# Order at the joints of an FFN: weighted sums ahead of the last gate quarter, half of them on TensorE, a half quarter ahead of the last token block

## The chip, the cores and the metric

The kernel runs on one core of a Trainium2 chip. The metric is the device time of one execution in microseconds (us). The engines are TensorE (PE; its weight loads are listed as PEld), VectorE (DVE), ScalarE (ACT), GpSimd (POOL) and SyncE (SP, which issues most of the DMA transfers).

## The reference

Two layers over 512 tokens of 1024 numbers, all float32. Each layer has a mixer (layer 0: a state-space mixer beside a pooling mixer; layer 1: stick-breaking attention) and then an FFN, which is what the change touches. Cut to what matters:

```
x   = layer_norm(ALPHA * x + mixer(x), ln_mix_g[i], ln_mix_b[i])
ple = (p[i] @ ple_w_proj[i]) * sigmoid(x @ ple_w_gate[i])
ffn = grouped_moe(x, ...)     # 16 SwiGLU experts in 4 groups, best group, best 2 experts in it
x   = layer_norm(ALPHA * x + ffn + ple, ln_ffn_g[i], ln_ffn_b[i])
```

In the mixture of experts each token goes to two experts, and the two results are summed with the weights (gates) that the router gave.

## The kernel before

The tokens stand in four blocks of 128 (`xt[0]` to `xt[3]`), each a tile of 128 x 1024. Every product with a weight is done in three matmuls (`mm3`, lines 87 to 89) on a high and a low part of both operands; the high part of a weight is made by ScalarE (L82) and the low part by VectorE (L83) from a raw tile that SP has loaded. The rows of the trace name the parts of a ring of such tiles `w_0h`, `w_0l`, `w_2l` and so on. Raw weights, the rows `yt` and the tile `yl` share a pool of slots; PSUM has four banks named A, two named B, two named T. A tile waits for the last reader of what stood in its slot or bank. Every engine carries out its instructions in one fixed order, which a list scheduler makes from the order in which the code emits them; nothing overtakes within an engine.

`ffn(layer, last)` goes as follows. For each token block, a POOL DMA writes it to DRAM (`xd`), PE transposes it (L168), and ACT and DVE split the transposed block into the tiles `cath`, `catl` (in layer 1 `oh`, `ol`). `logits` (L794, L795) puts the router's products for all blocks into one bank `pr`, and `route` (from L801 on) turns these on DVE into lists of tokens, gates and an index tile `ixm` (L913). With that index POOL gathers the rows of an expert (L934, tile `xg`), and `load_g` transposes them on PE (L994) and splits them into `g`. `up` and `down` are the two stages of an expert; there are 16.

Beside the experts stand four gate quarters, `gate_parts(c)`, each of 256 columns of the `ple` term and in two halves `b` of two token blocks: 48 matmuls into a bank `pG` (x times the gate weights), a sigmoid on ACT (L964), 12 matmuls into a bank `pB` (p times its weights, `pT`), the product of both on DVE (L968) and its addition to x (L972, L974). Two quarters stand at the start, ahead of the first expert, one among the experts, and the last, c = 3, at the end.

At the end SP loads the experts' results, two per token, from DRAM into `yt` (L1064; one tile of 1 MB for each token block). The last expert doesn't go that way: its result stays in SBUF as `yl` (high part by ACT, L1068, low part by DVE, L1069), and PE brings it to the tokens with a one-hot matrix (L1098, into an A bank). In each half of the last quarter, after the quarter's own work, DVE adds the two weighted `yt` rows of a block (L1085, the weighted sums), then the one-hot product from the A bank (L1100, which also sums up the rows for the layer norm), and `ln_finish` follows (L781 and L784 on DVE, a square on ACT, a power on POOL, L786 and L787 on DVE). In layer 1 alone, blocks 2 and 3 take their weighted sums on PE: four small copies on ACT (L1077) make diagonal matrices `dg` of the gates, and L1094 multiplies them with `yt` into the same bank.

After the first FFN comes the attention layer, which begins with the transposes of the four blocks and the value projection (pA <- w, x2T).

Of the kernel before, what the change touches and what calls it, by code (L numbers as in the profile page):

```python
# [11 lines left out]
AF = mybir.ActivationFunctionType  # L12
OP = mybir.AluOpType
AX = mybir.AxisListType

D = 1024
S = 512
NT = 4
# [3 lines left out]
NE = 16  # L22
CAP = 96
# [3 lines left out]
GATES = (-1, -1, 7, 15)  # L27
# [3 lines left out]
LF = 9  # L31
# [7 lines left out]
class Trunk:  # L39
# [875 lines left out]
    def ffn(self, layer, last):  # L915
        nc, v = self.nc, self.nc.vector
        xt = self.xt
        X = self.cat or self.xt_pair(f"x{layer}T")
        xd = self.dp.tile([S, D], F32, name=f"xd{layer}")
        yd = self.dp.tile([2 * S, D], F32, name=f"yd{layer}")  # L920
        pT = self.pT
        xgs = self.slot(f"xg{layer}").rearrange("p (a d) -> p a d", a=2)
        nc.gpsimd.memset(xgs, 0.0)
        pr = self.bank("B", "pB")
        for i in range(NT):
            nc.gpsimd.dma_start(xd[i * 128:(i + 1) * 128, :], xt[i])
            self.transposes(xt[i], i, X, "TA"[i % 2])
        for i in range(NT):
            self.logits(X, pr, i)
        self.prefetch(self.used + 2 * GATES.count(-1) + LF)  # L930
        self.route(pr, layer)

        def gather(e):
            return nc.gpsimd.indirect_dma_start(  # L934
                out=xgs[:CAP, e % 2, :], out_offset=None, in_=xd[:, :],
                in_offset=bass.IndirectOffsetOnAxis(ap=self.ix[:CAP, e:e + 1], axis=0),
                bounds_check=S - 1, oob_is_err=False)

        def scatter(e, src):
            nc.gpsimd.indirect_dma_start(  # L940
                out=yd[:, :], out_offset=bass.IndirectOffsetOnAxis(ap=self.iy[:CAP, e:e + 1], axis=0),
                in_=src[:CAP], in_offset=None, bounds_check=2 * S - 1, oob_is_err=False)

        with self.tc.issue_after(gather(0).ins):
            scatter(NE - 1, xgs[:, 1, :])
        gather(1)

        def ple(p, i, w):
            ts = slice(i * 128, (i + 1) * 128)
            for k in range(2):  # L950
                self.mm3(p, (pT[:, 0, k, ts], pT[:, 1, k, ts]), w[k], k == 0, k == 1)
# [3 lines left out]
        def gate_parts(c):  # L955
            w = self.weights(LA)
            wp = self.weights(LA)
            cs = slice(c * 256, (c + 1) * 256)
            for b in range(2):
                p = self.bank("A" if c < ng or c == 3 else "B", "pG").rearrange("p (i n) -> p i n", i=2)  # L960
                for i in range(2):
                    self.proj_x(p[:, i], 2 * b + i, X, w)
                sg = self.half4("sg")[:, :512].rearrange("p (i n) -> p i n", i=2)
                nc.scalar.activation(sg, p, AF.Sigmoid)  # L964
                p = self.bank("B", "pB").rearrange("p (i n) -> p i n", i=2)
                for i in range(2):
                    ple(p[:, i], 2 * b + i, wp)
                v.tensor_tensor(sg, sg, p, op=OP.mult)  # L968
                for i in range(2):
                    x = xt[2 * b + i][:, cs]  # L970
                    if c < 3:
                        v.scalar_tensor_tensor(x, x, ALPHA, sg[:, i], op0=OP.mult, op1=OP.add)  # L972
                    else:
                        v.tensor_tensor(x, x, sg[:, i], op=OP.add)  # L974
                    if c == 2:
                        x = xt[2 * b + i][:, 768:]
                        nc.scalar.activation(x, x, AF.Copy, scale=ALPHA)
                yield

        def gate(c):  # L980
            for _ in gate_parts(c):
                pass

        ng = GATES.count(-1)
        for c in range(ng):
            gate(c)

        def load_g(e):
            g = self.slot(f"g{layer}_{e}", F32R)[:, :2 * KB * CAP].rearrange("p (a k t) -> p a k t", a=2, k=KB)
            for hf in range(2):  # L990
                p = self.bank("T", "pT")[:, :4 * CAP]
                for k in range(4):
                    kb = hf * 4 + k
                    nc.tensor.transpose(p[:, k * CAP:(k + 1) * CAP], xgs[:CAP, e % 2, kb * 128:(kb + 1) * 128],  # L994
                                        self.ident[:CAP, :CAP])
                ks = slice(hf * 4, hf * 4 + 4)
                self.split(g[:, 0, ks], g[:, 1, ks], p.rearrange("p (k t) -> p k t", k=4))
            if e + 2 < NE:
                gather(e + 2)
            return g  # L1000

        def up(g, hh, kh, a, pool=False):
            w = self.weights(LA, pool)
            for k in range(4):
                kb = kh * 4 + k
                self.mm3(hh[a][:CAP], (g[:, 0, kb], g[:, 1, kb]), w[k], kb == 0, kb == KB - 1)
# [16 lines left out]
        def down(sT):  # L1023
            for nh in range(2):
# [3 lines left out]
                    self.mm3(py, (sT[:, 0, k], sT[:, 1, k]), w[k], k == 0, k == 3)  # L1028
                yield slice(nh * 512, (nh + 1) * 512), py

        g = load_g(0)
        hh = [self.bank("A", "pA"), self.bank("A", "pA")]
        up(g, hh, 0, 0)
        up(g, hh, 0, 1)
# [3 lines left out]
        for e in range(NE - 1):  # L1038
            LA = 6 if e < 13 else 3
            sg = act(hh)  # L1040
            hh = [self.bank("A", "pA"), self.bank("A", "pA")]
            up(gn, hh, 0, 0)
            sT = turn(sg)
            up(gn, hh, 0, 1)
            ysb = self.half4("ysb")
            for h, py in down(sT):
                nc.scalar.activation(ysb[:CAP, h], py, AF.Copy)  # L1047
            scatter(e, ysb)
            if e == OVER:
                self.overflow(layer, xd, yd)  # L1050
            if e == NE - 3:
                oht = self.last_onehot()
                self.ln_setup("ln_ffn", layer)
            if e in GATES:
                gate(GATES.index(e))
            g = gn
            if e + 2 < NE:
                gn = load_g(e + 2)
            up(g, hh, 1, 0)
            up(g, hh, 1, 1)  # L1060
        yts = []
# [5 lines left out]
        for h, py in down(turn(act(hh))):  # L1067
            nc.scalar.activation(yl[:CAP, 0, h], py, AF.Copy, scale=self.gs[:CAP])  # L1068
            v.scalar_tensor_tensor(yl[:CAP, 1, h], py, self.gs[:CAP], yl[:CAP, 0, h].bitcast(F32),  # L1069
                                   op0=OP.mult, op1=OP.subtract)  # L1070
        st = self.cp.tile([128, NT, 2], F32, tag="st", bufs=2, name=f"st{layer}f")
        onpe = (2, 3) if last else ()
        if onpe:
            dg = self.half4("dg").rearrange("p (x t) -> p x t", x=8)
            for n, i in enumerate(onpe):
                for k in range(2):
                    nc.scalar.activation(dg[:, 2 * n + k], self.ident, AF.Copy, scale=self.gates[:, k, i])  # L1077
        parts = gate_parts(3)
        for b in range(2):
            next(parts)  # L1080
            for i in (2 * b, 2 * b + 1):
                if i in onpe:
                    continue
                for k in range(2):
                    v.scalar_tensor_tensor(xt[i], yts[i][:, k * D:(k + 1) * D], self.gates[:, k, i], xt[i],  # L1085
                                           op0=OP.mult, op1=OP.add)
            for i in (2 * b, 2 * b + 1):
                for nh in range(2):
                    h = slice(nh * 512, (nh + 1) * 512)
                    p = self.bank("A", "pA")  # L1090
                    first = True
                    if i in onpe:
                        for k in range(2):
                            nc.tensor.matmul(p, dg[:, 2 * onpe.index(i) + k],  # L1094
                                             yts[i][:, k * D + nh * 512:k * D + (nh + 1) * 512], start=first, stop=False)
                            first = False
                    for a in range(2):
                        nc.tensor.matmul(p, oht[:CAP, i * 128:(i + 1) * 128], yl[:CAP, a, h], start=first, stop=(a == 1))  # L1098
                        first = False
                    v.scalar_tensor_tensor(xt[i][:, h], p, 1.0, xt[i][:, h], op0=OP.mult, op1=OP.add,  # L1100
                                           accum_out=st[:, i, nh:nh + 1])
                self.ln_finish(xt[i], st[:, i], f"{layer}f{i}")
                if last:
                    nc.sync.dma_start(self.out[i * 128:(i + 1) * 128, :], xt[i])
# [202 lines left out]
```

## Time and profile before

| | |
|---|---|
| median of 3 runs | 1246.93 us (1245.92 to 1250.49) |
| the profiled execution | 1245.8 us |
| its span, first to last instruction | 1244.1 us |
| mean granted TensorE clock | 0.976 |
| busy share PE, DVE, ACT, POOL | 94%, 78%, 60%, 11% |

Idle time of PE is the difference between its busy time and the span. A timeline row gives the start, the time of one or of a merged group, the engine, the line, the operation, what it writes and reads, and in brackets how long the engine stood idle before it and what ended that. Matmuls overlap one another, so the distance of their starts is the pace, not the time of one.

### The profile page before, as it was taken

To read this page: it belongs to the slowest core of one execution; us is meant where nothing else is said; L and a number is where in the kernel's file an instruction comes from. 1 tells how busy PE (TensorE), PEld (TensorE's weight loads), DVE (VectorE), ACT (ScalarE), POOL (GpSimd) and SP (SyncE) were. 2 spreads that over 40 slices of the span, in tenths; PEclk is the share of its full clock that TensorE was granted. 3 is DMA by queue.
4 is the path that set the end of the run, shared out by engine and by line. 5 is a ranking of instruction groups with operands and counts; after the bars stand their busy time and mean duration, and the time that the engine had idled before them with its cause. 6 is when DMAs were issued, how large, how long until landed. Compare 5 with 4: busy or idle time off the path is not lost.

```text
span 1244.1 us, 17404 instructions
## 1 busy us (share of the span) xinstructions
PE 1164.7 (94%) x6463; PEld 891.8 (72%) x6463; DVE 966.0 (78%) x1385; ACT 749.7 (60%) x1059; POOL 136.5 (11%) x150
## 2 busy tenths in 40 slices
PE   6977999999999999987999999998999999998985
PEld 4867779777768776676777767688877768776763
DVE  6997866798886989776576467758599886998765
ACT  4312542688876888742465446523588885888751
POOL 5010021011100110100000000011101110011101
PEclk9988999999999999988999999999999999999998
DMA  7225653599996998952122024434399997999851
GB/s 251 68 79 180 234 217 121 187 371 385 383 379 226 381 387 305 329 227 83 35 67 70 1 69 157 155 143 149 110 359 383 378 373 256 349 388 333 315 216 69
DMA packets 158167, 285.15 MB, mean 229 GB/s; under 512 B 19584, under 2 KB 43664, under 8 KB 157008
## 3 DMA queue, kind: packets, MB, share of 16 engines
q1 hardware_dynamic: 143760, 256.56, 57.9%
q0 software_dynamic: 9568, 25.19, 5.9%
q10 hardware_dynamic: 4736, 2.10, 0.6%
q8 instruction: 56, 0.92, 0.3%
q14 instruction: 47, 0.39, 0.1%
HBM read 272.02 MB, written 20.19 MB: 235 GB/s over the span
## 4 chain that ended last, share of the span: by engine, by line
PE 40%; DVE 8%; DMA 4%; issue 2%; ACT 1%; POOL 0%; POOLq 0%; ACTq 0%; DVEq 0%
PE pA L89 8%; PE pA L88 8%; PE pA L87 8%; DMA xg<-xd,ixm 3%; DVE kw L679 2%; PE pB L89 2%; PE pB L88 2%; PE pB L87 2%; PE pA L691 2%; PE pG L87 1%; PE pG L88 1%; PE pG L89 1%; DVE kw L680 1%; PE pT L686 1%; PE pT L994 1%
## 5 line engine op out<-in xcount | busy, mean ns | idle before, releaser
L83 DVE TENSOR_TENSOR w_0l<-raw,w_0h 128x1024 fp32r<-128x1024 f32 (+1 forms) x233 | 280.0, 1202 | 61.9 <-ACT w_0h L82 57.5
L82 ACT ACTIVATE w_0h<-raw 128x1024 fp32r<-128x1024 f32 (+1 forms) x233 | 242.5, 1041 | 62.4 <-PE pG L89 33.9
L83 DVE TENSOR_TENSOR w_2l<-raw,w_2h 128x1024 fp32r<-128x1024 f32 x205 | 249.8, 1219 | 18.0 <-ACT w_2h L82 17.7
L82 ACT ACTIVATE w_2h<-raw 128x1024 fp32r<-128x1024 f32 x205 | 216.5, 1056 | 52.4 <-PE pA L89 43.1
L87 PE MATMUL pA<-w_0h,g 128*96 128x512 f32 x256 | 104.3, 407 | 2.4 <-ACT g L82 2.4
L88 PE MATMUL pA<-w_0l,g 128*96 128x512 f32 x256 | 100.9, 394 | 1.8 <-DVE w_0l L83 1.8
L89 PE MATMUL pA<-w_0h,g 128*96 128x512 f32 x256 | 101.8, 398 | 0.9 <-DVE g L83 0.9
L89 PE MATMUL pA<-w_2h,g 128*96 128x512 f32 x256 | 101.6, 397 | 0.0
L87 PE MATMUL pA<-w_2h,g 128*96 128x512 f32 x256 | 101.2, 395 | 0.0
L88 PE MATMUL pA<-w_2l,g 128*96 128x512 f32 x256 | 100.9, 394 | 0.0
L940 POOL DMA_INDIRECT yd<-ysb,ixm x30 | 37.7, 1257 | 444.6 <-ACT ysb L1047 422.4
L89 PEld LDWEIGHTS pA<-w_0h,g 128*96 128x96 f32 x256 | 41.2, 161 | 19.9 <-DVE g L83 3.1
L934 POOL DMA_INDIRECT xg<-xd,ixm x32 | 38.9, 1215 | 145.2 <-PE pT L994 91.8
L88 PEld LDWEIGHTS pA<-w_2l,g 128*96 128x96 f32 x256 | 41.6, 163 | 18.0
L89 PEld LDWEIGHTS pA<-w_2h,g 128*96 128x96 f32 x256 | 41.4, 162 | 18.1
L87 PEld LDWEIGHTS pA<-w_0h,g 128*96 128x96 f32 x256 | 41.5, 162 | 17.6 <-ACT g L82 4.6
L87 PEld LDWEIGHTS pA<-w_2h,g 128*96 128x96 f32 x256 | 41.3, 162 | 17.7
L88 PEld LDWEIGHTS pA<-w_0l,g 128*96 128x96 f32 x256 | 41.5, 162 | 17.4 <-DVE w_0l L83 3.8
L87 PE MATMUL pB<-w_0h,sT 128*96 128x512 f32 x128 | 50.9, 397 | 1.2 <-ACT sT L82 1.2
L89 PE MATMUL pB<-w_0h,sT 128*96 128x512 f32 x128 | 51.2, 400 | 0.0
L88 PE MATMUL pB<-w_0l,sT 128*96 128x512 f32 x128 | 50.7, 396 | 0.4 <-DVE w_0l L83 0.4
L679 DVE TENSOR_TENSOR_SCAN kw<-kw 128x128 f32<-128x128 f32 (+3 forms) x64 | 50.3, 813 | 0.9 <-ACT kw L676 0.6
(442 smaller groups left out, 2812.6 us busy)
## 6 DMA issues: line engine op xcount, KB each, us to landing
raw<-in_moe_w_dram SPq DMA_DIRECT2D x192, 1024.0 KB, 10.1
raw<-in_sb_w_qkv_dram SPq DMA_DIRECT2D x12, 1024.0 KB, 9.4
raw<-in_ple_w_gate_dram SPq DMA_DIRECT2D x8, 1024.0 KB, 10.8
yt<-yd SPq DMA_DIRECT2D x8, 1024.0 KB, 7.1
raw<-in_ab_w_out_dram SPq DMA_DIRECT2D x4, 1024.0 KB, 5.7
xd<-x0r POOLq DMA_DIRECT2D x8, 512.0 KB, 4.2
raw<-in_sb_w_out_dram SPq DMA_DIRECT2D x4, 1024.0 KB, 6.1
raw<-in_ab_w_in_dram SPq DMA_DIRECT2D x3, 1024.0 KB, 7.3
```

The lines of the kernel that those rows point to most:

```text
L82: return (self.nc.scalar.activation(hi, src, AF.Copy), (self.nc.gpsimd if pool else self.nc.vector).tensor_tensor(lo, src, hi.bitcast(F32) ...
L83: (self.nc.gpsimd if pool else self.nc.vector).tensor_tensor(lo, src, hi.bitcast(F32), op=OP.subtract))
L87: t.matmul(out, s[0], m[0], start=first, stop=False)
L88: t.matmul(out, s[0], m[1], start=False, stop=False)
L89: t.matmul(out, s[1], m[0], start=False, stop=last)
L679: v.tensor_tensor_scan(rv, rv, rv, 1.0, op0=OP.mult, op1=OP.min)
L680: v.tensor_tensor(sg[:, :n - 1], sg[:, :n - 1], kp[:, 1:n], op=OP.mult)
L686: nc.tensor.transpose(pT[:, ks], sg[:, ks], self.ident)
L691: nc.tensor.matmul(po[s * 64:s * 64 + 64, qs], vs[:, kb, hc:hc + 64], kw[s][:, kb * 128:(kb + 1) * 128], start=(kb == 0), stop=(kb == qb))
L934: return nc.gpsimd.indirect_dma_start(out=xgs[:CAP, e % 2, :], out_offset=None, in_=xd[:, :], in_offset=bass.IndirectOffsetOnAxis(ap=self. ...
L940: nc.gpsimd.indirect_dma_start(out=yd[:, :], out_offset=bass.IndirectOffsetOnAxis(ap=self.iy[:CAP, e:e + 1], axis=0), in_=src[:CAP], in_of ...
L994: nc.tensor.transpose(p[:, k * CAP:(k + 1) * CAP], xgs[:CAP, e % 2, kb * 128:(kb + 1) * 128], self.ident[:CAP, :CAP])
```

## The change

There are four edits, all in `ffn`. At the start, `gate_parts(0)` is opened early: its first half is emitted ahead of the last token block's transposes, each block's logits directly follow its transposes, and the second half comes after the first two gathers. The first half of quarter 1 is emitted ahead of `load_g(0)`, its second half after it. At the end, the weighted sums of blocks 0 and 1 are emitted ahead of quarter 3, and blocks 2 and 3 take theirs on PE in both layers. The second half of quarter 3 puts its `pG` into a B bank.

```
-        pr = self.bank("B", "pB")
-        for i in range(NT):
-            nc.gpsimd.dma_start(xd[i * 128:(i + 1) * 128, :], xt[i])
-            self.transposes(xt[i], i, X, "TA"[i % 2])
-        for i in range(NT):
-            self.logits(X, pr, i)
-        self.prefetch(self.used + 2 * GATES.count(-1) + LF)
-        self.route(pr, layer)
...
-                p = self.bank("A" if c < ng or c == 3 else "B", "pG").rearrange("p (i n) -> p i n", i=2)
+                p = self.bank("A" if c < ng or (c == 3 and b == 0) else "B", "pG").rearrange("p (i n) -> p i n", i=2)
...
         ng = GATES.count(-1)
-        for c in range(ng):
-            gate(c)
+        pr = self.bank("B", "pB")
+        early = gate_parts(0)
+        for i in range(NT):
+            nc.gpsimd.dma_start(xd[i * 128:(i + 1) * 128, :], xt[i])
+            if i == NT - 1:
+                next(early)
+            self.transposes(xt[i], i, X, "TA"[i % 2])
+            self.logits(X, pr, i)
+        self.prefetch(self.used + 2 * ng - 2 + LF)
+        self.route(pr, layer)
...
+        for _ in early:
+            pass
...
+        early = gate_parts(1)
+        next(early)
         g = load_g(0)
+        for _ in early:
+            pass
...
-        onpe = (2, 3) if last else ()
-        if onpe:
-            dg = self.half4("dg").rearrange("p (x t) -> p x t", x=8)
-            for n, i in enumerate(onpe):
+        onpe = (2, 3)
+        dg = self.half4("dg").rearrange("p (x t) -> p x t", x=8)
+        for n, i in enumerate(onpe):
+            for k in range(2):
+                nc.scalar.activation(dg[:, 2 * n + k], self.ident, AF.Copy, scale=self.gates[:, k, i])
+        for i in range(NT):
+            if i not in onpe:
                 for k in range(2):
-                    nc.scalar.activation(dg[:, 2 * n + k], self.ident, AF.Copy, scale=self.gates[:, k, i])
+                    v.scalar_tensor_tensor(xt[i], yts[i][:, k * D:(k + 1) * D], self.gates[:, k, i], xt[i],
+                                           op0=OP.mult, op1=OP.add)
         parts = gate_parts(3)
         for b in range(2):
             next(parts)
-            for i in (2 * b, 2 * b + 1):
-                if i in onpe:
-                    continue
-                for k in range(2):
-                    v.scalar_tensor_tensor(xt[i], yts[i][:, k * D:(k + 1) * D], self.gates[:, k, i], xt[i],
-                                           op0=OP.mult, op1=OP.add)
```

Three places show how the edits move instructions. Line numbers shift with the change: L968 becomes L944, L972 and L974 become L948 and L950, L1069 becomes L1074, L1094, L1098 and L1100 become L1097, L1101 and L1103; the weighted sum keeps L1085.

First, VectorE at the end of the first FFN, from the last weight split of the tail on (`x0r_1245` holds blocks 0 and 1, `yt_0` the rows of block 0). Before:

```order
L83 TENSOR_TENSOR w_0l<-raw_5291,w_0h 128x512
L1069 SCALAR_TENSOR_TENSOR yl_5279<-pB,gs,yl_5279 96x512 x2
L968 TENSOR_TENSOR sg<-sg,pB 128x512
L974 TENSOR_TENSOR x0r_1245<-x0r_1245,sg 128x256 x2
L1085 SCALAR_TENSOR_TENSOR x0r_1245<-yt_0_5271,gates_1696,x0r_1245 128x1024
L1085 SCALAR_TENSOR_TENSOR x0r_1245<-yt_1_5273,gates_1696,x0r_1245 128x1024
```

The same place in the changed kernel:

```order
L1085 SCALAR_TENSOR_TENSOR x0r_1245<-yt_0_5271,gates_1775,x0r_1245 128x1024
L83 TENSOR_TENSOR w_0l<-raw_5291,w_0h 128x512
L1085 SCALAR_TENSOR_TENSOR x0r_1245<-yt_0_5271,gates_1775,x0r_1245 128x1024
L1085 SCALAR_TENSOR_TENSOR x0r_1245<-yt_1_5273,gates_1775,x0r_1245 128x1024 x2
L1074 SCALAR_TENSOR_TENSOR yl_5279<-pB,gs,yl_5279 96x512 x2
L1103 SCALAR_TENSOR_TENSOR x0r_1245,st0f<-pA,x0r_1245 128x512
L944 TENSOR_TENSOR sg<-sg,pB 128x512
```

The four sums stand ahead of `yl` and of the gate quarter's product, and the first add from PSUM stands ahead of that product.

Second, TensorE at the same place, from the one-hot products of blocks 0 and 1 on (`pB_5512` is the second half's p product, `pG_5461` its gate product). Before:

```order
L1098 MATMUL pA_5429<-yl0_5279,oht_5052 128x512 x2
L1098 MATMUL pA_5433<-yl0_5279,oht_5052 128x512 x2
L1098 MATMUL pA_5445<-yl0_5279,oht_5052 128x512 x2
L1098 MATMUL pA_5449<-yl0_5279,oht_5052 128x512 x2
L87 MATMUL pB_5512<-w113_0h_5354,pT0_1258 128x256
L88 MATMUL pB_5512<-w113_0l_5355,pT0_1258 128x256
```

In the changed kernel, there and behind the last of the second half's p products:

```order
L1101 MATMUL pA_5450<-yl0_5279,oht_5052 128x512 x2
L1101 MATMUL pA_5454<-yl0_5279,oht_5052 128x512 x2
L87 MATMUL pG_5466<-w112_0h_5353,cath0_1175 128x256
L88 MATMUL pG_5466<-w112_0l_5354,cath0_1175 128x256
L89 MATMUL pG_5466<-w112_0h_5353,catl0_1176 128x256
```

```order
L89 MATMUL pB_5517<-w113_0h_5363,pT0_1258 128x256
L1097 MATMUL pA_5533<-yt0_2_5275,dg_5342 128x512 x2
L1101 MATMUL pA_5533<-yl0_5279,oht_5052 128x512 x2
L1097 MATMUL pA_5539<-yt0_2_5275,dg_5342 128x512 x2
L1101 MATMUL pA_5539<-yl0_5279,oht_5052 128x512 x2
```

The gate products of the second half now come ahead of its p products, and each of the four A banks of blocks 2 and 3 first gets two products with `dg` (L1097).

Third, VectorE at the start of the first FFN (`pT_1545`, `pT_1552` before and `pT_1680`, `pT_1687` after are the transposes of the last token block; `pB_1498` holds the router's products). Before:

```order
L787 SCALAR_TENSOR_TENSOR x0r_1_1248<-x0r_1_1248,mv0m3_1486,ln_mix0_1251 128x1024
L83 TENSOR_TENSOR catl1_914<-pT_1522,cath1_913 128x4x128
L83 TENSOR_TENSOR catl0_1176<-pT_1530,cath0_1175 128x4x128
L83 TENSOR_TENSOR catl1_914<-pT_1537,cath1_913 128x4x128
L83 TENSOR_TENSOR catl0_1176<-pT_1545,cath0_1175 128x4x128
L83 TENSOR_TENSOR catl1_914<-pT_1552,cath1_913 128x4x128
L83 TENSOR_TENSOR w12_4l_1894<-raw12_1338,w12_4h_1893 128x1024
L801 COPY rt_1641<-pB_1498 32x512
```

After:

```order
L83 TENSOR_TENSOR w12_4l_1894<-raw12_1338,w12_4h_1893 128x1024
L83 TENSOR_TENSOR catl0_1176<-pT_1562,cath0_1175 128x4x128
L83 TENSOR_TENSOR catl1_914<-pT_1569,cath1_913 128x4x128
L944 TENSOR_TENSOR sg_1662<-sg_1662,pB_1664 128x512
L948 SCALAR_TENSOR_TENSOR x0r_0_1245<-x0r_0_1245,sg_1662 128x256 x2
L83 TENSOR_TENSOR catl0_1176<-pT_1680,cath0_1175 128x4x128
L83 TENSOR_TENSOR catl1_914<-pT_1687,cath1_913 128x4x128
L801 COPY rt_1720<-pB_1498 32x512
```

The first half quarter's product and addition stand ahead of the last token block's splits, which follow its transposes.

## Rows read from the trace of the kernel before

**Rows 1.** Page, busy us, share of the span and instructions of TensorE:

```profile
PE 1164.7 (94%) x6463; PEld 891.8 (72%) x6463; DVE 966.0 (78%) x1385; ACT 749.7 (60%) x1059; POOL 136.5 (11%) x150
```

**Rows 2.** Waits of PE, whole span: in total, times, longest us:

```profile
PE pG L87 <- DVE x0r L1100: 7.5, 2, 3.8
PE pA L87 <- DVE x0r L1100: 6.3, 1, 6.3
```

**Rows 3.** Timeline of DVE, end of the last FFN:

```profile
1199.17 0.68 DVE L83 TENSOR_TENSOR w_0l<-raw,w_0h 128x512 fp32r<-128x512 f32 x1
...
1201.07 0.75 DVE L1069 SCALAR_TENSOR_TENSOR yl<-pB,gs,yl 96x512 fp32r<-96x512 f32 x1 [0.56 <-ACT yl L1068]
1207.61 0.69 DVE L968 TENSOR_TENSOR sg<-sg,pB 128x512 f32<-128x512 f32 x1 [5.80 <-PE pB L89]
...
1209.02 4.86 DVE L1085 SCALAR_TENSOR_TENSOR x0r<-yt,gates,x0r 128x1024 f32<-128x1024 f32 x4
```

**Rows 4.** Timeline of PE, same stretch, up to the tail's last groups:

```profile
1207.34 2.00 PE L1098 MATMUL pA<-yl,oht 96*128 96x512 f32 x8
1209.18 0.28 PE L87 MATMUL pB<-w_0h,pT 128*128 128x256 f32 x1
...
1210.50 0.28 PE L89 MATMUL pB<-w_0h,pT 128*128 128x256 f32 x1
1214.54 0.42 PE L87 MATMUL pG<-w_0h,oh 128*128 128x256 f32 x1 [3.76 <-DVE x0r L1100]
...
1221.88 1.88 PE L1094 MATMUL pA<-yt,dg 128*128 128x512 f32 x4
...
1224.07 1.88 PE L1094 MATMUL pA<-yt,dg 128*128 128x512 f32 x4
```

**Rows 5.** Timeline of DVE, last add and last norm operation of the kernel:

```profile
1232.24 0.68 DVE L1100 SCALAR_TENSOR_TENSOR x0r<-pA,x0r 128x512 f32<-128x512 f32 x1
...
1236.36 1.28 DVE L787 SCALAR_TENSOR_TENSOR x0r<-x0r,mv1f,ln_ffn 128x1024 f32<-128x1024 f32 x1 [0.44 <-POOL mv1f L785]
```

**Rows 6.** Timeline of DVE, end of the first FFN:

```profile
542.52 0.69 DVE L968 TENSOR_TENSOR sg<-sg,pB 128x512 f32<-128x512 f32 x1 [5.79 <-PE pB L89]
...
560.28 4.86 DVE L1085 SCALAR_TENSOR_TENSOR x0r<-yt,gates,x0r 128x1024 f32<-128x1024 f32 x4
...
567.02 0.68 DVE L1100 SCALAR_TENSOR_TENSOR x0r<-pA,x0r 128x512 f32<-128x512 f32 x1
...
573.38 1.27 DVE L787 SCALAR_TENSOR_TENSOR x0r<-x0r,mv0f,ln_ffn 128x1024 f32<-128x1024 f32 x1
```

**Rows 7.** Timeline of PE, first matmul of the value projection:

```profile
565.90 0.76 PE L87 MATMUL pA<-w_0h,x2Th 128*128 128x512 f32 x1 [6.35 <-DVE x0r L1100]
```

**Rows 8.** Timeline of ACT, the diagonal matrices of layer 1:

```profile
1194.64 1.26 ACT L1077 ACTIVATE dg<-ident,gates 128x128 f32<-128x128 f32 x4
```

**Rows 9.** Timeline of PE, start of the first FFN:

```profile
185.67 0.23 PE L795 MATMUL pB<-catl,rwa 128*16 128x128 f32 x1 [1.43 <-DVE catl L83]
186.86 1.55 PE L168 MATMUL pT<-ident,x0r 128*128 128x128 f32 x8 [0.96 <-DVE x0r L787]
```

**Rows 10.** Windows: busy us (instructions) of each engine, granted clock, DMA share, GB/s:

```profile
187.00:191.00 4.00, 4.00 (x36) 3.96 (x36) 3.93 (x6) 1.35 (x3) 0.57 (x1) 0.57 0.77 176
```

**Rows 11.** Timeline of DVE, first step of the router:

```profile
192.28 0.68 DVE L801 COPY rt<-pB 32x512 f32<-32x512 f32 x1 [1.35 <-PE pB L795]
```

**Rows 12.** Timeline of POOL, first gather of the first FFN:

```profile
207.50 1.07 POOL L934 DMA_INDIRECT xg<-xd,ixm  x1 [19.82 <-DVE gates L887]
```

**Rows 13.** Tile xg, 200 to 240 us: time from issue to landing:

```profile
DMA to landing us min/median/max: 4.1/4.8/7.5
```

**Rows 14.** Timeline of PE, gathered rows and first expert matmul:

```profile
224.63 0.83 PE L994 MATMUL pT<-ident,xg 96*128 96x96 f32 x8
226.31 0.47 PE L87 MATMUL pA<-w_0h,g 128*96 128x512 f32 x1 [0.86 <-ACT g L82]
```

**Rows 15.** Windows, end of the last FFN's loads; columns as in rows 10:

```profile
1202.00:1204.00 2.00, 2.00 (x19) 2.00 (x19) 0.00 (x0) 0.34 (x1) 0.00 (x0) 1.00 0.30 123
```

More of the change, by code (lines that the diff above doesn't have):

```diff
@@ L923, in ffn @@
         nc.gpsimd.memset(xgs, 0.0)
-        pr = self.bank("B", "pB")
-        for i in range(NT):
-            nc.gpsimd.dma_start(xd[i * 128:(i + 1) * 128, :], xt[i])
-            self.transposes(xt[i], i, X, "TA"[i % 2])
-        for i in range(NT):
-            self.logits(X, pr, i)
-        self.prefetch(self.used + 2 * GATES.count(-1) + LF)
-        self.route(pr, layer)
[L933 to L946, printed above, removed]
         def ple(p, i, w):
@@ L984, in ffn, with gather, scatter @@
         ng = GATES.count(-1)
-        for c in range(ng):
-            gate(c)
+        pr = self.bank("B", "pB")
[8 more added lines that the diff above has]
+        self.route(pr, layer)
+        def gather(e):
+            return nc.gpsimd.indirect_dma_start(
+                out=xgs[:CAP, e % 2, :], out_offset=None, in_=xd[:, :],
+                in_offset=bass.IndirectOffsetOnAxis(ap=self.ix[:CAP, e:e + 1], axis=0),
+                bounds_check=S - 1, oob_is_err=False)
+        def scatter(e, src):
+            nc.gpsimd.indirect_dma_start(
+                out=yd[:, :], out_offset=bass.IndirectOffsetOnAxis(ap=self.iy[:CAP, e:e + 1], axis=0),
+                in_=src[:CAP], in_offset=None, bounds_check=2 * S - 1, oob_is_err=False)
+        with self.tc.issue_after(gather(0).ins):
+            scatter(NE - 1, xgs[:, 1, :])
+        gather(1)
+        for _ in early:
+            pass
         def load_g(e):
```

## The prediction

> **What bounds the kernel now.** I read the busy shares first. TensorE (PE) works 1164.7 of 1244.1 us [rows 1], so what an edit of order can return is PE's idle time, 79.4 us, and what runs at half clock behind it. The waits of PE come next [rows 2]. Three of the longest have one releaser, L1100, VectorE's (DVE's) add of the PSUM result into the token block: 3.8 us in each of the two FFN tails at the second half of gate quarter 3 (pG L87), and 6.3 us at the join to the attention layer (pA L87). The FFN starts have small waits of their own, which I come to below.
>
> The tail of the last FFN shows how the 3.8 arises. DVE finishes its part of the last expert's result at 1201.07+0.75 = 1201.8, then stands idle 5.80 us until pB gives L968 something, and only then does the four weighted sums, 4.86 us from 1209.02 [rows 3]. PE has put the one-hot products of blocks 0 and 1 into all four A banks by 1209.2, does 12 matmuls that need none, and stops at 1210.6 until L1100 frees a bank [rows 4]. The 48 matmuls from 1214.54 start at 0.42 us each against 0.28 before, and take until 1221.88, 7.34 us; at the pace of 0.12 before the stop (1209.18 to 1210.50 in 11 steps) they are 5.76. So the wait costs 3.8 and half clock 1.6.
>
> **End of the last FFN.** Removed: DVE's order L968, L974, sums. The sums now fill the idle stretch. From 1199.17 DVE has one sum (pace 4.86/4 = 1.2), the 0.6 us split of w_0l that stood there, three sums, and the two yl of 0.65: 1199.2+4.9+0.6+1.3 = 1206.0. PE needs yl at 1207.34 [rows 4]; 1.3 us are spare, and the first ple matmul, which needs the bank that the first yl frees, is due 12 x 0.12 before 1207.34, at 1205.9, 0.6 after that yl's end at 1205.3. So L1100's four adds start when the one-hot products are there, beside PE's next 48+12 matmuls. The second half takes a B bank, whose reader is yl, done. PE then goes on without a stop: 1209.18 + 60 x 0.12 = 1216.4 in place of 1221.88, **5.5 us** earlier. What follows is the same on PE: four groups of 2.19 (1221.88 to 1224.07). DVE has the layer norms of blocks 0 and 1 done by my chain at about 1218 (adds from 1208, then L968 and L974, then norms of 2.4 a block), ahead of the first group's end, 1218.6, so the last add keeps its distance to them, as do the 4.1 us from it to the last norm operation [rows 5]. Low end 3.8, the wait alone, should half clock come at another place of the tail; high end 5.5.
>
> **End of the first FFN.** The first 5.5 are alike: L968 waits 5.79 [rows 6] on an idle DVE. Blocks 2 and 3 change too. Their sums, 4.86 on DVE from 560.28, become four groups of PE work, of which 4 x 1.73 = 6.9 us are new (2.19 less two one-hot products at 1.84/8). PE: the one-hot products of blocks 0 and 1 end at 544.1 (as in the last FFN 1.6 after L968's start), 60 x 0.12 later it is 551.3, and 4 x 2.19 later 560.05. Without the new groups PE stood idle from 559.5 for 6.35 us [rows 7], so the new work costs PE nothing as long as DVE is the later of the two. DVE then adds with a pace set by PE's groups, the last add starting about 561.0. The norm behind it took 7.6 from the add's start to its end here (567.02 to 574.65) and 5.4 in the last FFN (1232.24 to 1237.64): 568.6 to 566.4 in place of 574.65, 6.0 to 8.2 earlier. Value **7.0**, the middle, since only part of the splits still lie between; low end 5.4, where half clock comes back after the waits of 0.4 and 1.6 us that my chain leaves on PE, high end 8.2. ScalarE gets four small copies, 1.26 us together [rows 8], needed at 551.3, long after the expert's last weight split; they hide in its waits for PE. The DMA queue of SP keeps its order; the slots it waits for come free with the sums, which end earlier.
>
> **The two FFN starts.** Each has two edits. The half quarter (48 pG, 12 pB) goes ahead of the last block's transposes; in the order only two pG and three pB lie in the waits for catl, and 39 pG and 9 pB come behind block 2's logits, ahead of block 3's transposes. Block 3 was ready at 186.86, where the 0.96 wait for it ended [rows 9]; so the 48 matmuls stand in no wait. On PE this is a sum of zero, plus the waits for block 1's catl: 2.2+1.2 by my chain against 1.43+0.96, **1.0** more. Behind them the clock was 0.57 for 4 us [rows 10], a loss of 4 x 0.43 = 1.7, which I keep.
>
> The router starts later: 48 x 0.12 = 5.8, 1.0 of waits, and an estimated 1.6 because block 3's logits now follow their own transposes and splits, where block 2's logits stood between: L801 [rows 11] goes from 192.28 to about 200.7, **8.4** later. Three weight splits now lie inside its chain on DVE (0.6 and two of about 1.2), of which those in DVE's waits for PE cost nothing: the gather is 8.4 to 11.3 later. Now it goes at 207.50 [rows 12] and lands in 4.1 at the fastest [rows 13], but its transposes start only at 224.63 [rows 14]: 13.0 spare. The second edit draws the transposes forward by the 17 pG and 12 pB placed behind them, 29 x 0.12 = 3.5; PE itself is 1.0 later; 10.5 are spare. PE then waits 0 to 0.8 for the rows, and gets back the 0.86 it now stalls for the split of g, which the 29 matmuls cover. With the 1.0 that is 0.1 to 0.9, **+0.5** a start; ends -2 (no wait for catl, no half clock, less than a full gain since the gather then bounds) and +3.9 (the landing at the 7.5 of its slowest row, 3.4 more).
>
> **Sum**, against the profiled execution's own 1245.8 us: -5.5 - 7.0 + 2 x 0.5 = -11.5, **1234 us**. The median of the runs, 1246.93, is 1.1 above that execution, so read against it the same sum is 1235.
>
> A weighing of the clock: the granted clock is 0.57 behind two waits of 1.43 and 0.96 with one matmul between [rows 9, 10]. The Trainium skill, "TensorE: Matmul & The Clock Gate", section "HAM oscillation — how this bites in real kernels", says that a kernel whose matmuls come in short bursts between waits falls back to the low clock at each, and that joining the work into longer stretches cures it. For the tails rule and rows agree; at the starts it speaks for the rival "clock held" below, since five more matmuls stand in the waits.
>
> **Rivals.**
> 1. *Slow gather.* The landing takes 7.5 instead of 4.1 [rows 13]: +3.9 a start: -12.5 + 7.8 = -4.7, 1241. For it: 10.5 spare against a delay of 8.4 to 11.3, no cover left. Against: 7.5 is the slowest of four.
> 2. *yt lands late.* DVE takes its instructions in order, so a sum that waits for yt holds yl and with it PE. The four loads of 1 MB end with the traffic, about 0.6 us into the stretch of [rows 15]; if they land together at 1202.6, the first yl ends at 1202.6+3 x 1.2+1.2+0.6+0.65 = 1208.6, 2.7 too late for ple, and at most as much is lost in the first FFN, where I take half: 1238. Against: they are issued in order, and blocks 0 and 1 are half of the bytes.
> 3. *Join gives its gain back.* The attention start waits for something else (weights, the norm's chain): only the last FFN's 5.5 remain, 1241.
> 4. *Clock held.* The two half-clock spells of the starts vanish, 1.7 each: 1234.3 - 3.4 = 1231. For it: more matmuls in the waits. Against: the order shows only five.
> 5. *Slower.* The stretch from L801 to the first expert matmul, 34.0 us (192.28 to 226.31), is a chain and not a pile of PE work: then all of 8.4 and up to 2.9 of splits are added at each start: -12.5 + 2 x 8.4 = +4.3, 1250; with the splits +10, 1256. It decides, as slower than now, from 6.3 lost a start. Against: in that stretch PE works through the gate quarters, and the gathered rows lie unread for 13.
> 6. *The change doesn't do what it says.* For the first edit the order already says so (five matmuls in the wait); that is priced in above.
>
> **How the numbers follow.** Forecast 0.50, with its own range 1230 to 1239 (tails -9.2 to -13.7, starts -2 to +2 together); slow gather 0.13; late yt 0.12; join 0.10; clock held 0.10; slower 0.05. About 0.5%, 6.2 us, is what a measurement tells from no change: under 1240.7 counts as faster. Forecast, clock held and late yt lie below it (0.72), slow gather and the join at its edge, so half of each: 0.83, which I round to 0.82 faster. The other halves and the mild end of the slower rival make 0.14 for no change, its other end 0.04 slower. The range 1227 to 1242 takes in all but the slower rival and the tails of the others.
>
> **What would show it.** Right: in the profile after, no wait of PE for the add at pG, the second half of quarter 3 at 0.28 us each, DVE's first sum at about 1199 of the old time; the pA wait of 6.3 down to about 2; L801 8 us later at each start, first expert matmul within 1 us. Wrong: a wait of DVE for yt, of PE for xg over 3 us, or of the value projection for weights; the last would mean that the join's 7.0 was never there.

## The result, and the profile after

| | before | changed |
|---|---|---|
| median of 4 runs | 1248.11 us (1245.92 to 1250.49) | 1232.70 us (1230.46 to 1233.94) |
| profiled execution / its span | 1245.8 / 1244.1 us | 1232.3 / 1230.7 us |
| mean granted clock | 0.976 | 0.985 |

The ratio is 0.9874, 95% interval 0.9849 to 0.9899: faster by 1.3%. The forecast was 1234 us, range 1227 to 1242. The profiled executions differ by 13.5 us; the working had given 11.5. The medians differ by 15.4, since the profiled execution of before was quicker than all four of its runs. That difference turns out to matter below.

VectorE at the end of the last FFN after the change, against [rows 3] and [rows 5]:

```profile
1191.27 1.28 DVE L1085 SCALAR_TENSOR_TENSOR x0r<-yt,gates,x0r 128x1024 f32<-128x1024 f32 x1
1192.46 0.68 DVE L83 TENSOR_TENSOR w_0l<-raw,w_0h 128x512 fp32r<-128x512 f32 x1
1193.07 3.79 DVE L1085 SCALAR_TENSOR_TENSOR x0r<-yt,gates,x0r 128x1024 f32<-128x1024 f32 x3
1196.78 1.40 DVE L1074 SCALAR_TENSOR_TENSOR yl<-pB,gs,yl 96x512 fp32r<-96x512 f32 x2
1200.12 0.69 DVE L1103 SCALAR_TENSOR_TENSOR x0r<-pA,x0r 128x512 f32<-128x512 f32 x1 [1.95 <-PE pA L1101]
...
1218.85 0.68 DVE L1103 SCALAR_TENSOR_TENSOR x0r<-pA,x0r 128x512 f32<-128x512 f32 x1
...
1222.97 1.28 DVE L787 SCALAR_TENSOR_TENSOR x0r<-x0r,mv1f,ln_ffn 128x1024 f32<-128x1024 f32 x1 [0.44 <-POOL mv1f L785]
```

The sums fill the stretch in which DVE stood idle for 5.80 us. None of them waits for yt, and yl is done at 1198.2. The 4.1 us from the last add to the last norm operation are unchanged. TensorE in the same stretch, against [rows 4]:

```profile
1199.45 2.00 PE L1101 MATMUL pA<-yl,oht 96*128 96x512 f32 x8
1201.29 0.28 PE L87 MATMUL pG<-w_0h,oh 128*128 128x256 f32 x1
...
1208.49 1.88 PE L1097 MATMUL pA<-yt,dg 128*128 128x512 f32 x4
```

There is no wait ahead of pG, and its first matmul takes 0.28 us instead of 0.42. From the one-hot products to the first group it is 9.04 us; in [rows 4] it was 14.54. That is the 5.5 of the working.

The join behind the first FFN, TensorE, against [rows 7]:

```profile
559.34 0.50 PE L87 MATMUL pA<-w_0h,x2Th 128*128 128x512 f32 x1 [0.25 <-ACT x2Th L82]
561.43 0.76 PE L168 MATMUL pT<-ident,x0r 128*128 128x128 f32 x4 [1.36 <-DVE x2Tl L83]
```

The wait of 6.35 us ahead of the value projection is down to 0.25. The 1.36 behind it was 1.28 before.

The start of the first FFN, TensorE, against [rows 9] and [rows 14]:

```profile
185.03 0.23 PE L795 MATMUL pB<-catl,rwa 128*16 128x128 f32 x1 [2.06 <-DVE catl L83]
...
186.82 0.29 PE L795 MATMUL pB<-catl,rwa 128*16 128x128 f32 x1 [1.03 <-DVE catl L83]
...
222.53 0.85 PE L995 MATMUL pT<-ident,xg 96*128 96x96 f32 x8 [1.03 <-DMA xg<-xd,ixm]
...
226.73 0.39 PE L87 MATMUL pA<-w_0h,g 128*96 128x512 f32 x1
```

The two waits for catl add up to 3.1 us (forecast 3.4), the wait for the gathered rows is 1.0 (forecast 0 to 0.8), and the wait for the split of g, 0.86 before, is gone. The router on VectorE and the gather on POOL (against [rows 11, 12]) are late as forecast, 200.66 against "about 200.7" and 218.14:

```profile
200.66 0.68 DVE L801 COPY rt<-pB 32x512 f32<-32x512 f32 x1 [0.68 <-PE pB L795]
```

```profile
218.14 1.07 POOL L973 DMA_INDIRECT xg<-xd,ixm  x1 [31.10 <-DVE gates L887]
```

To see where 13.4 us of span went, I cut both traces at events that both have: a DMA of POOL in each mixer (127 and 772 us of before), and in each FFN the scatter of its first expert and the first one-hot product. "after again" is a second execution (experiments).

| stage (length before) | after | after again | worked out |
|---|---|---|---|
| start of span (127.2) | -0.65 | -0.42 | 0 |
| start of FFN 1 (124.2) | +0.31 | +0.38 | +0.5 |
| experts of FFN 1 to its one-hot products (290.9) | -1.64 | -0.30 | 0 |
| end of FFN 1 and attention (229.5) | -5.54 | -7.05 | -7.0 |
| start of FFN 2 (142.7) | +1.34 | +1.46 | +0.5 |
| experts of FFN 2 (292.8) | -1.71 | -0.82 | 0 |
| end of FFN 2 (36.7) | -5.50 | -5.50 | -5.5 |

The two executions of one program differ by 0.9 to 1.5 us in three stages. The granted clock says why. Half clock is the lower of TensorE's two levels, 1.2 of 2.4 GHz: 0.50 in a row that lies inside such a stretch (187 to 189 us in "after"), and a mean between 0.5 and 1 in a wider one. Two windows, first in "after", then in "after again" (columns as in [rows 10]):

```profile
561.00:566.00 5.00, 4.57 (x17) 3.88 (x18) 5.00 (x7) 2.33 (x4) 1.45 (x1) 0.66 0.32 97
528.00:532.00 4.00, 4.00 (x17) 2.63 (x18) 3.65 (x4) 3.75 (x7) 0.00 (x0) 1.00 1.01 422
```

```profile
561.00:566.00 5.00, 3.64 (x19) 2.89 (x20) 5.00 (x10) 2.85 (x5) 1.04 (x1) 1.00 0.04 6
528.00:532.00 4.00, 3.80 (x11) 2.51 (x11) 3.16 (x5) 3.12 (x6) 0.00 (x0) 0.57 1.01 426
```

The half clock stood at the attention's start in the one and among the last experts in the other. A stretch of it takes 4 x 0.43 = 1.7 us of PE's work; in the stage times above it costs 1.3 to 1.5 us.

### The profile page after: what moved, and what is told of

Read it like the earlier page. It is cut to its first block, busy times and chain, and to the rows that moved or that the text cites. A ratio compares the mean times of both kernels' runs of the same rounds, so it can differ in the third digit from the quotient of the medians.

```text
span 1230.7 us, 17431 instructions
## 1 busy us (share of the span) xinstructions
PE 1162.8 (94%) x6479; PEld 888.6 (72%) x6479; DVE 959.1 (78%) x1381; ACT 750.9 (61%) x1063; POOL 134.9 (11%) x150
```

## The experiments

Each run is compared with runs of the kernel before on the same chip. ends_only, starts_only, after_again and block0 shared one chip (before: 1248.7), ends_late, block0_late, sums_dve and bank_a another (1250.0), and the last two pairs a third, in two sittings (1247.7 and 1247.8).

**ends_only.** The starts as in the kernel before, the ends as changed:

```
-        early = gate_parts(0)      # and with it all edits at the start
+        for c in range(ng):
+            gate(c)
```

> Only the edits at the FFN ends (sums first, blocks 2 and 3 on TensorE, B bank); the FFN starts as in the kernel before. My theory: the gain is all from the ends, 5.5 us in the last FFN and 5.5 to 7.0 at the join, and the starts cost about 1 in all; so this is 1 to 2 us below the changed kernel, 1229 to 1233 us, with L801 at 192 and the first expert matmul at 225.7 to 226.3. Rival (the starts gain): it is 2 us or more above the changed kernel. Third theory, on the clock: stretches at half clock outside the edited places (before: 528 to 533 and 1149 to 1154, 1.7 us each) come and go between kernels and shift each by 1.7.

Measured 1238.85, ratio 0.9914 (0.9892 to 0.9936): not 1229 to 1233. The ends carry most of the gain, and yet the kernel with the start edits is 6.7 us quicker. My first theory fell. Even the profile, the quickest of the six executions (1236.1), holds a piece of it. At the start of the second FFN, ScalarE, VectorE and TensorE:

```profile
850.89 0.42 ACT L977 ACTIVATE x0r<-x0r 128x256 f32<-128x256 f32 x1 [6.78 <-DMA xd<-x0r]
851.21 0.21 ACT L822 ACTIVATE rt<-pT 128x64 f32<-128x64 f32 x1
```

```profile
846.31 0.67 DVE L801 COPY rt<-pB 32x512 f32<-32x512 f32 x1
851.45 0.23 DVE L823 TENSOR_TENSOR rt<-rt,rbias 128x64 f32<-128x64 f32 x1 [4.46 <-ACT rt L822]
```

```profile
857.36 0.18 PE L865 MATMUL pT<-mb,tri 128*128 128x16 bf16 x1 [3.50 <-DVE mb L859]
```

L977 scales the last 256 columns of x. The code emits it with gate quarter 2, the scheduler hoists it, and for the last token block it must wait until POOL's write of that block to xd has read x. L822, the router's second step, stands behind it on ScalarE; `mb`, the mask of the chosen experts, is what the router gives PE next. In the kernel before, first profile, the same place reads 1.90 us of waiting for L822, and only 0.86 for mb:

```profile
857.91 0.23 DVE L823 TENSOR_TENSOR rt<-rt,rbias 128x64 f32<-128x64 f32 x1 [1.90 <-ACT rt L822]
```

There the clock was at half from 849 to 853, L801 came 4.9 us after the write's issue (855.34 and 850.41), and the write landed 6.9 us after it; in ends_only L801 came 3.7 us after the issue (842.58), and the write took 8.2.

**starts_only.** The other half:

```
-        onpe = (2, 3)
+        onpe = (2, 3) if last else ()
...                                  # sums again behind each half of quarter 3, pG in an A bank
```

> Only the edits at the FFN starts; the ends as in the kernel before. My theory: 0 to 3 us above the kernel before (+0.3 to +0.5 of waits a start, one spell of half clock, 1.7, where it falls so), with both 3.8 us waits of PE for the add and the 6.3 at the join still there. Rival (the starts gain): 2 us or more below the kernel before.

1245.73, ratio 0.9979 (0.9962 to 0.9996): about 2.6 us faster, which is the rival's side. In its profile L823 waits 1.6 us for L822 and no ScalarE wait for xd shows: L801 stands 9 us later (201.36, and 865.37 in the second FFN), and by then the write has landed (194.04 and 856.80). The profile doesn't show the 2.6 us at the starts, though: against the first profile of before they are 0.2 and 1.6 us longer, and the experts behind them, where that profile had half clock at 528 and 1149 and this one has none, 1.1 shorter in each FFN.

**ends_late** tests that reading without the start edits: L977's scale factor becomes a tile computed from the gates, so L977 cannot stand ahead of L822.

```
+        al = self.cp.tile([128, 1], F32, tag="al", bufs=2, name=f"al{layer}")
+        v.tensor_scalar(al, self.gates[:, 0, 0], 0.0, ALPHA, op0=OP.mult, op1=OP.add)
...
-                        nc.scalar.activation(x, x, AF.Copy, scale=ALPHA)
+                        nc.scalar.activation(x, x, AF.Copy, scale=al)
```

> The kernel with the edits at the ends only, and ScalarE's scaling of the last 256 columns of x (L977) tied to the gates, so that it can no longer stand ahead of the router's copy L822. In ends_only L977 of the last block waits 6.8 us for that block's write to xd, L822 stands behind it, VectorE waits 4.5 for L822, and TensorE 3.5 for mb. My new theory: this queue on ScalarE is what the start edits save (they move the router 8 us later, when the write has landed). Then the wait of L823 for L822 falls under 1.5 us, PE's wait for mb under 1, and the time falls from 1238.9 to that of the changed kernel, 1231 to 1234 us. Rival (the start edits gain elsewhere, in PE's order): it stays at 1237 to 1240 us.

1233.43, ratio 0.9867 (0.9841 to 0.9892), the time of the changed kernel (0.9855, 0.9874). The wait of L823 is 1.63, not under 1.5; 1.6 is also what it is in the traces of the changed kernel and of block0. VectorE and TensorE at the same place:

```profile
848.69 0.68 DVE L801 COPY rt<-pB 32x512 f32<-32x512 f32 x1 [0.90 <-PE pB L795]
850.99 0.23 DVE L823 TENSOR_TENSOR rt<-rt,rbias 128x64 f32<-128x64 f32 x1 [1.63 <-ACT rt L822]
```

```profile
856.91 0.18 PE L865 MATMUL pT<-mb,tri 128*128 128x16 bf16 x1 [0.58 <-DVE mb L859]
```

The stage "start of FFN 2" fell from +2.86 to -0.07 against before, with one stretch of half clock in each of the three. So taking the queue away brings the time of the changed kernel without its start edits. That this queue is all that the start edits bring is not shown: the traces have 2.9 us of it at the second start and 0.3 at the first, while the medians differ by 5.4, and none of the slower executions of ends_only was profiled. Nor do the two kernels gain in the same stages: at the second start ends_late is 1.4 us ahead of the changed kernel (-0.07 and +1.34), in the experts of FFN 2 it is 2.9 behind (+1.18 and -1.71).

**before_late** and **before_again.** The late scaling alone on the kernel before, and that kernel's second profile.

> The kernel before with nothing changed but the late scaling (L977 tied to the gates). If the write to xd that ScalarE waits for ahead of L822 costs the kernel before in most executions (and little in the one profiled, where PE's wait for mb was 0.9), this gives what the start edits alone gave or more: 2 to 5 us below the kernel before, with a narrower spread of its times. Rival (the write costs only where TensorE runs at full clock at that place, as in ends_only): within 1.5 us of the kernel before.

> The kernel before once more, for its profile: whether the waits of VectorE at L823 for L822 (1.9 us twice in the first profile) and of TensorE for mb (0.8 and 0.9) are the same in another execution. If the landing of xd varies from execution to execution, one of them differs by 1 us or more; a stretch at half clock outside the FFN ends and the attention's start moves as well.

before_late: 1246.12, ratio 0.9981 (0.9961 to 1.0001), 1.5 us in the medians and 2.4 by the ratio. The interval takes in 1, so this alone is not told from no change, and it doesn't decide between my theory (2 to 5 us) and the rival (within 1.5). Its times spread no less (1239.6 to 1249.7). before_again shows the variation: at the second start

```profile
858.53 0.42 ACT L977 ACTIVATE x0r<-x0r 128x256 f32<-128x256 f32 x1 [6.39 <-DMA xd<-x0r]
```

```profile
865.00 0.18 PE L865 MATMUL pT<-mb,tri 128*128 128x16 bf16 x1 [3.10 <-DVE mb L859]
```

The wait for mb is 3.1 where the first profile had 0.9, with the clock full from 849 to 856, L801 3.7 us after the write's issue instead of 4.9, and xd landing after 7.8 us instead of 6.9. The stage "start of FFN 2" is 2.5 us longer than in the first profile. In these three traces the write is nearly hidden where half clock slows PE ahead of the router, and costs 2.5 to 2.9 us of PE's wait where it doesn't (0.6 is left of that wait in ends_late, without the queue).

**after_again.** The changed kernel unchanged.

> The changed kernel once more. If half-clock stretches belong to the program, they stand where they stood (186 to 190, 561 to 566, 841 to 849, none at 528 or 1149) and each stage keeps its length within 0.3 us. If they hang on a phase that differs from execution to execution, one of them at least moves, and a stage changes by 1.7 us.

1232.13, ratio 0.9855 (0.9832 to 0.9879). Half clock moved in part: the stretches at the two FFN starts stayed (187 to 190, 842 to 849), the one at 561 went, and others came at 528 and 1187.

**sums_dve.** The sums of blocks 2 and 3 in the first FFN on VectorE:

```
-        onpe = (2, 3)
+        onpe = (2, 3) if last else ()
```

The emission of the changed kernel then puts all eight weighted sums ahead of quarter 3, not at their old place.

> The changed kernel with the sums of blocks 2 and 3 of the first FFN back on VectorE, at their old place behind the second half of gate quarter 3; all else as changed. By the working of the join: the new groups on TensorE cost it nothing, VectorE gets 4.86 us of sums back, of which the groups' 6.9 us of work no longer stand ahead; the value projection waits for the add again. Forecast 1 to 4 us slower than the changed kernel, 1233 to 1236 us, PE's wait at pA 3 to 6 us. Rival (sums ahead are all of the gain, the sums on TensorE only trade): the same as the changed kernel within 1 us.

1231.90, ratio 0.9860 (0.9835 to 0.9885): the same as the changed kernel, the rival's value. TensorE at the join:

```profile
550.59 2.00 PE L1102 MATMUL pA<-yl,oht 96*128 96x512 f32 x8
552.94 1.09 PE L168 MATMUL pT<-ident,x0r 128*128 128x128 f32 x8 [0.36 <-DVE x0r L787]
...
559.83 1.12 PE L168 MATMUL pT<-ident,x0r 128*128 128x128 f32 x4 [4.55 <-DVE x2Tl L83]
```

PE saves the 6.9 us of L1097 and waits 4.55 for VectorE instead. The 4.86 of sums went to an earlier place on VectorE (those of blocks 2 and 3 start from 539.93 to 544.23; in [rows 6] at 560.28). So it doesn't matter here which engine takes them, as long as they stand ahead; those of blocks 2 and 3 on VectorE at their old place, with the other four early, were not run.

**bank_a.** `self.bank("A" if c < ng or c == 3 else "B", "pG")` as before, all else as changed.

> The changed kernel with the second half of quarter 3 in an A bank as before; TensorE's order is the same. In the trace of the changed kernel the first add L1103 reads its A bank from 1200.12 to 1200.8 and TensorE starts the second half at 1201.29, so the bank would be free 0.5 us earlier than needed. My theory: no change within 1 us, 1231 to 1233. Rival (the own bank carries the tail's gain): a wait of TensorE for L1103 at pG of 1 us or more in each tail, and half clock behind it, 2 to 6 us slower.

1233.03, ratio 0.9871 (0.9844 to 0.9897), the same. No wait of PE for L1103 in its trace:

```profile
1198.36 2.00 PE L1101 MATMUL pA<-yl,oht 96*128 96x512 f32 x8
1200.20 0.28 PE L87 MATMUL pG<-w_0h,oh 128*128 128x256 f32 x1
```

Once the sums are early, the first add empties an A bank in time, and the own bank is worth nothing. It was undone alone, and not together with the sums on PE.

**block0, block0_late** and their repeats. The first half quarter in two pieces, token block 0's behind block 0's logits, since the piece that waits for block 1's catl cannot fill the wait for it:

```
                 for i in range(2):
                     self.proj_x(p[:, i], 2 * b + i, X, w)
+                    if c == 0 and 2 * b + i == 0:
+                        yield
...
-            if i == NT - 1:
-                next(early)
             self.transposes(xt[i], i, X, "TA"[i % 2])
             self.logits(X, pr, i)
+            if i == 0:
+                next(early)
```

> The changed kernel with the first half of quarter 0 opened in two pieces: token block 0's 24 gate products are emitted behind block 0's logits, block 1's 24 and the 12 p products behind the last block's logits. Block 0's products need nothing of block 1, for whose catl PE waits 2.1 and 1.0 us at each start. My theory (the half quarter was late because half of it needs block 1): the waits at a start fall from 3.1 to under 1.5, the half-clock stretch shrinks or goes, L801 stands 2 to 4 us after that of the kernel before and not 8.4: 2 to 4 us a start less than the changed kernel, 1225 to 1229 us. Rival (VectorE sets the length of the start, PE's work only fills it): L801 at the same time or the first expert matmul at the same time as in the changed kernel, no gain.

> block0 with the same late scaling. In block0 the waits of ScalarE for xd are 3.2 us in total, 1.8 at the longest. If they cost something there, up to 1.8 a start: 1223 to 1226 us. If they are hidden by TensorE's gate products, as PE's small wait for mb of 1.1 in all says: the same as block0, 1225 to 1227 us.

> block0 once more, beside block0_late on one chip. Its first run gave 1226.0, block0_late on another chip 1229.5, though the starts have the same length in both profiles (to 0.1 us). If the late scaling does nothing here, both now give the same within 2 us, 1225 to 1230. Rival (the late scaling costs): block0_late is 3 us or more slower again.

> The same pair. Late scaling without effect: within 2 us of block0_again. Rival: 3 us or more slower, and then some stage of its profile must be longer for another reason than half clock.

block0: 1225.97, ratio 0.9809 (0.9786 to 0.9832); again 1225.59, 0.9834. It beats both kernels, the changed one by 6.2 us on the same chip. TensorE at the first start:

```profile
187.42 0.23 PE L795 MATMUL pB<-catl,rwa 128*16 128x128 f32 x1 [1.38 <-DVE catl L83]
...
192.58 0.23 PE L795 MATMUL pB<-catl,rwa 128*16 128x128 f32 x1 [0.48 <-DVE catl L83]
```

The waits for catl fall from 3.1 to 1.9, the granted clock of 185 to 190 is 1.00 (0.66 in the changed kernel), L801 stands at 193.20, and the start of FFN 1 is 2.1 us shorter than before instead of 0.3 longer; that of FFN 2 is 2.0 shorter. My count of waits (under 1.5) was too good. Of the 2.4 us by which its first start beats the changed kernel's, 1.1 are waits of PE (all of them together: 3.6 us instead of 4.7); the rest is about what a stretch of half clock costs there (bank_a, at half clock there from 185 to 193 where the changed kernel is so from 186 to 190, is 1.2 us longer in this stage).

The late scaling added to it costs instead of helping: 1229.54 and 1229.44 (0.9840, 0.9867). The starts are as long as block0's to 0.1 us; the experts of FFN 2 take 3.5 to 4.1 us longer. Both of its profiles have half clock at 1137 to 1144 and at 1182 to 1188, block0's two have neither; right ahead of the first, PE waits for VectorE's queue at L1139, the branch for overfull experts, 3.0 and 2.9 us; in block0 it is 1.4 and 2.0. Why that wait is longer there I did not find.

## Why the prediction was right, and where not

The forecast of 1234 us came within 1.3 of the median, in part by luck. In the profiles the two ends give 11.0 us where the sum had 12.5, the starts cost 1.6 where it had 1.0, and 4.0 come from stages that it had at nothing (0.65 ahead of the first FFN, 1.64 and 1.71 in the experts).

- **End of the last FFN, 5.5:** right in size and by its own steps (5.50 in both executions).
- **End of the first FFN, 7.0:** the size held (5.5 with a stretch of half clock left, 7.05 without), but the step "blocks 2 and 3 to PE, off VectorE" brought nothing: sums_dve has the sums on VectorE and the same time. By the traces, what works is that the sums leave the path behind the last gate half: the waits of 3.8 and 6.35 go (0.25 is left of the second), and with them most of the half clock behind (549 to 553 and 563 to 573 us of before; 562 to 565 after).
- **B bank:** a part of the change that I carried inside the 5.5; by bank_a it is worth nothing once the sums are early.
- **The starts, +0.5 each:** the wrong step. Against the first profile of before TensorE's sum held: +0.3 in the first FFN and +1.3 in the second, where the changed kernel has two stretches of half clock (0.57 from 841 to 849); sums_dve, with the same start and one stretch (0.79), has -0.2. L801, the waits for catl, the gather and its 1 us wait came nearly as worked out. What the sum lacks is ScalarE: L822 behind L977 behind the write to xd. I let the router of before begin with L801 as if its chain had a fixed length, and looked at PE's wait for mb of 0.8 and 0.9 in one execution. Others pay 3.1 and 3.5. So the start edits don't cost 1.0, they gain: 2.6 us alone, 6.7 beside the new ends in the medians. The traces show this queue costing L823 0.5 us (first profile of before) to 3.2 us (ends_only) in the two starts together; where the rest of the 6.7 arises stays open. The edit at quarter 1 was never undone alone.
- **Rivals:** the gather came 10.6 us late and its rows 1.0, so *slow gather* was near but did not decide (no start in any trace waits longer for these rows). *yt lands late* did not occur: in the last FFN the rows of blocks 0 and 1 landed at 1187.9 and 1190.8, and the first sum starts at 1191.27 without a wait. *Join gives its gain back* did not either: 5.5 and 7.05 there. *Clock held* was not this change's doing; in block0 it is. *Slower* fell with the gather.
- The other 2 us between 11.5 and 13.4 in the profiles are half clock at 528 and 1149, which the profiled execution of before had and that of after had not, against one stretch more at the second start and one left at the join. The one at 1149 stands behind a wait of PE of 3.3 us at the branch for overfull experts, which was 2.0 in the changed kernel; I had priced none of this. It is no chance of one execution: all five profiles without the start edits have a stretch there (1143 to 1157), and of the nine with them only sums_dve and the two of block0_late; where a kernel was profiled twice, both agree. The wait alone doesn't make it, since starts_only waits 3.6 us there and keeps full clock. So a part of what the start edits bring may lie here; no run separates it.

The Trainium skill's page "TensorE: Matmul & The Clock Gate" (section "HAM oscillation — how this bites in real kernels") advises to restructure a kernel whose matmuls come in short bursts between waits, so that the work runs on and TensorE keeps its clock. The trace of block0 agrees: with 22 gate matmuls ahead of the wait for block 1's catl, where the changed kernel has two gate and three p matmuls, the clock of 185 to 190 us is 1.00 instead of 0.66. The page's case has longer waits than the 2.06 and 1.03 us here.

## What to carry to other kernels

Before pricing a step that moves, look at every engine's queue at its place, not only at the engines it runs on: an instruction hoisted ahead of a chain can hold it by a DMA that the profiled execution happened to hide. To fill a wait, move only work that does not need what the wait is for. And when several edits come together, undo each: at the ends, the sums on PE and the own bank could each be undone without loss, which leaves the place of the sums.

## What was not expected of the hardware

Some stretches at half clock come and go between executions of one program (561 and 528 in the two traces above), while others stand in both (187 and 842 there). One costs less than its 1.7 us of work: at the second start the changed kernel with two is 1.5 us longer than sums_dve with one. They also hide other waits: the landing of a 512 KB write, 6.9, 7.8 and 8.2 us at one place in three traces, left TensorE waiting 0.9 us behind half clock and 3.1 to 3.5 without it.
